# Key selection of a sparse attention layer: three query tiles searched each by itself with ScalarE counting and GpSimd keeping the bound, the other three in groups on VectorE

## The chip, the core and the metric

The kernel runs on one core of one Trainium2 chip. The core's engines are TensorE (PE, matmuls; PEld is its weight load), VectorE (DVE), ScalarE (ACT), GpSimd (POOL) and SyncE (SP, which issues transfers). Each engine takes its instructions in the order in which the program lists them, and waits at the first whose inputs are not there. The metric is the time of one execution on the device in microseconds, the median of several runs.

## What is computed

A decoder trunk of two layers over 1024 positions of 1024 features, in float32. The change lies in the second layer, a sparse attention: for each query an indexer scores all earlier keys, the 256 best are kept, and 16 heads attend to those alone.

```python
topk = min(TOPK_MAX, S // 4)                      # 256
...
rel = jax.nn.relu(jnp.einsum('bqhd,bkd->bqhk', qib, kif))
score = jnp.einsum('bqhk,bqh->bqk', rel, wib)
score = jnp.where(causal[None], score, -jnp.inf)
_, idx = lax.top_k(score, topk)
...
p = jax.nn.softmax(s, axis=-1)                    # over the selected keys
o = jnp.einsum('bqgjk,bqkgd->bqgjd', p, v_sel)
```

## The kernel before

**Tiles.** Queries are cut into eight tiles of 128. Query tile t sees (t+1)·128 keys, so tiles 0 and 1 need no selection (they have no more than 256 keys), and tiles 2 to 7 do, over 384 to 1024 keys.

**The search.** `index_tile(t)` computes the scores `sc_t` (128 queries by n keys). `topk` then finds, for each query, the 256th largest score by a binary search on the bits of the float: 16 steps on the high half word (`hw_t` holds it, int16), some work in between that puts the low half words of the keys at the threshold into `hw_t` (L1280 to L1297), and 16 steps on the low half (uint16). One step counts the keys above a bound `c2`, writes whether the count meets the limit (`hit`), and moves the bound. A count is either one VectorE instruction with an accumulator (L1236, output `jk`) or one ScalarE instruction, the sign of key minus bound with a sum (L1254, also into `jk`). The rest of a step is three small instructions on 128x(number of tiles): GpSimd takes half the step off the old bound (`cm`, L1249), VectorE compares the counts with the limit (L1260) and adds both (L1262; L1264 after the last step). After both searches each tile is finished on VectorE: a count, the two comparisons with the threshold (L1317, L1318), a running sum for ties (L1320), L1323 and L1326. L1326 writes the tile's mask into `hw_t`.

**Groups and where they count.** Tiles are searched in groups that share the small instructions. Group [3, 2] is searched early, while the scores of tiles 4 to 7 are computed, all of it on VectorE. Groups [7, 5] and [6, 4] come later, step by step in turn. In the first search of these ScalarE counts tiles 7 and 5 and VectorE 6 and 4; in the second ScalarE counts 7 and 4, and VectorE 5 and 6. VectorE does the small instructions of all groups.

**What lies around it.** TensorE has other work meanwhile: the scores (L1187), the query and key projections (`pj_qo`, `pj_ko`), which a fill queue spreads over the stage, the values `V_o`, and then the attention in units (query tile, key group, head pair). A unit of query tile t is named `o<t>_..`: scores `s_o` on TensorE, a masked row maximum on VectorE (L336, `st_o`), the exponential on ScalarE (L342), a scaling on GpSimd (L350), transposes `tp_o` on TensorE, their split into a high part on ScalarE (`ph_o`) and a low part on VectorE (`pl_o`), the product with the values, and the output's copies on ScalarE (L859, L861: `ah_o`, `a_o`), addition on GpSimd (L862) and split (`aoH` on ScalarE, `aoL` on GpSimd). The units of query tiles 0 and 1 need no mask from the search; those of tile 7 come next and need `hw_7` as L1326 leaves it, then the other tiles. The output weight is split into `woH` (ScalarE) and `woL` (VectorE or GpSimd); `held["sign"]` holds the first `woH` back until the last recorded sign is done. L1448 adds the attention's output to the residual.

**What sets the order.** The code is written in the order in which work is wanted; a scheduler that simulates the engines' times then fixes each engine's list. So a change of the search moves the instructions of everything around it as well. `topk` is a generator, one `yield` for each step, and the caller says which group steps when:

```python
    soon = topk([3, 2], ((), ()), 2, True)
...
    first, second = topk(TKA, TKACT, 0), topk(TKB, TKACT, 1)
    for _ in soon:
        next(first)
        next(second)
    while next(first, first) is not first:
        next(second)
    run(second)
```

## Time and profile before

| | us |
|---|---|
| median of three runs | 2592.92 (2591.56 to 2593.54) |
| the profiled execution, its own time | 2583.69 |
| its span in the trace | 2581.5 |
| TensorE busy | 2415.7 (94%) |
| VectorE busy | 1919.4 (74%) |
| ScalarE busy | 1275.2 (49%) |
| GpSimd busy | 937.9 (36%) |

The shares are averages over the whole span. The key selection lies between about 1339 and 1640 us, and there the picture is another: it has to be read from windows of that stretch. Rows further down give starts in us from the beginning of the span, then a duration, the engine, the line of the kernel, and what is written from what.

### The profile page before, as it was taken

What the parts mean: (1) busy time and instruction counts of PE and PEld (TensorE: products, weight loads), DVE (VectorE), ACT (ScalarE), POOL (GpSimd) and SP (SyncE); (2) the same over time, 40 slices, a digit from 0 to 9 for tenths busy, and PEclk for the clock granted to TensorE, in tenths of its full rate; (3) what the DMA queues carried; (4) which work ended last, traced back from release to release, by engine and by line L of the source; (5) the groups of instructions that cost most, each with busy time, mean ns of one, the idle gap of its engine ahead of it and who ended that gap; (6) DMA issues with size and microseconds to landing.
All of it is one profiled execution on the core that took longest, in us unless ns stands there. A gap on an engine that the chain in (4) does not pass through costs nothing.

```text
span 2581.5 us, 36095 instructions
## 1 busy us (share of the span) xinstructions
PE 2415.7 (94%) x12152; PEld 2024.3 (78%) x12152; DVE 1919.4 (74%) x3711; ACT 1275.2 (49%) x2395; POOL 937.9 (36%) x830
## 2 busy tenths in 40 slices
PE   8999999997999999999897886899988999999998
PEld 7888798886778877888686665799876788788887
DVE  5377765788665668788669999888856766688886
ACT  4354455555454453333434457777754544543333
POOL 2243344534333333244046434534441332324440
PEclk9999999998999999999999987999998999999999
DMA  7555565715254467542352334212342444684431
GB/s 256 157 172 150 156 187 150 216 34 200 89 175 135 149 239 253 163 147 98 114 136 70 110 108 90 82 50 74 83 176 94 165 149 150 213 317 147 146 115 66
DMA packets 160953, 373.14 MB, mean 145 GB/s; under 512 B 19329, under 2 KB 56449, under 8 KB 159745
## 3 DMA queue, kind: packets, MB, share of 16 engines
q1 hardware_dynamic: 160768, 370.85, 44.7%
q8 instruction: 96, 1.57, 0.3%
q14 instruction: 89, 0.72, 0.1%
HBM read 246.51 MB, written 123.73 MB: 143 GB/s over the span
## 4 chain that ended last, share of the span: by engine, by line
PE 71%; DVE 14%; DMA 6%; issue 4%; ACT 3%; POOL 1%; SPq 1%; DVEq 0%; POOLq 0%; ACTq 0%
PE dnA L702 13%; PE dnB L702 10%; PE upB L569 8%; PE pj_e L144 5%; PE upC L569 5%; PE upA L569 5%; PE o L144 4%; DVE jk L1236 3%; PE oo L144 3%; PE v L144 3%; PE tp_o L367 2%; PE dn_oe L144 2%; PE tp L367 2%; DMA K<-qk 1%; PE s L335 1%
## 5 line engine op out<-in xcount | busy, mean ns | idle before, releaser
L702 PE MATMUL dnA<-db,da 128*128 128x512 f32 x1536 | 354.5, 390 | 0.9 <-ACT db L100 0.9
L672 POOL TENSOR_TENSOR wr<-wr,wr 128x1024 f32<-128x1024 f32 x64 | 208.6, 3289 | 362.8 <-DVE db L101 319.5
L702 PEld LDWEIGHTS dnA<-db,da 128*128 128x128 f32 x1536 | 288.0, 188 | 62.9 <-ACT db L100 1.3
L702 PE MATMUL dnB<-db,da 128*128 128x512 f32 x1152 | 270.5, 395 | 5.7 <-DVE xd L709 5.7
L100 ACT CAST db<-wr 128x1024 fp32r<-128x1024 f32 x112 | 112.1, 1047 | 317.9 <-PE dnB L702 136.0
L702 PEld LDWEIGHTS dnB<-db,da 128*128 128x128 f32 x1152 | 217.9, 189 | 55.6 <-issue 6.1
L569 PE MATMUL upA<-B,wc 128*128 128x512 f32 x768 | 196.0, 403 | 11.5 <-ACT m L587 4.2
L101 DVE TENSOR_TENSOR da<-hr,da 128x1024 fp32r<-128x1024 f32 x112 | 187.5, 1706 | 19.4 <-ACT da L100 19.4
L569 PE MATMUL upB<-T,wc 128*128 128x512 f32 x768 | 187.8, 393 | 0.0
L569 PEld LDWEIGHTS upA<-B,wc 128*128 128x128 f32 x768 | 146.6, 192 | 48.6 <-ACT m L587 5.3
L101 DVE TENSOR_TENSOR wc<-ru,wc 128x512 fp32r<-128x512 f32 x148 | 125.5, 855 | 74.0 <-ACT wc L100 69.0
L536 POOL TENSOR_TENSOR ws<-ru 128x512 f32<-128x512 f32 x32 | 46.0, 1438 | 363.5 <-DMA ru<-in_ffn_up_dram 201.9
L101 DVE TENSOR_TENSOR db<-wr,db 128x1024 fp32r<-128x1024 f32 x112 | 164.8, 1510 | 14.3 <-ACT db L100 13.5
L100 ACT CAST wc<-ru 128x512 fp32r<-128x512 f32 x160 | 97.4, 619 | 157.1 <-DMA hid<-s 32.7
L569 PEld LDWEIGHTS upB<-T,wc 128*128 128x128 f32 x768 | 144.1, 188 | 32.7
L350 POOL TENSOR_SCALAR st_o<-st_o,am_o 128x128 f32<-128x128 f32 (+7 forms) x128 | 103.9, 814 | 137.2 <-DVE am_o L345 79.6
L342 ACT ACTIVATE st<-st,am 128x896 f32<-128x896 f32 (+7 forms) x128 | 99.3, 776 | 77.9 <-DVE am L336 76.2
L100 ACT CAST da<-hr 128x1024 fp32r<-128x1024 f32 x112 | 112.6, 1045 | 43.0 <-DMA hr<-hid 43.0
L350 POOL TENSOR_SCALAR st<-st,am 128x896 f32<-128x896 f32 (+3 forms) x96 | 74.7, 780 | 152.3 <-DVE am L345 145.6
L1236 DVE TENSOR_SCALAR_CACHE_REDUCE jk<-hw,tkf 128x512 bf16<-128x512 uint16 (+7 forms) x140 | 117.5, 865 | 1.0
L709 DVE TENSOR_TENSOR xd<-xd,dnA 128x512 f32<-128x512 f32 x128 | 84.7, 680 | 42.6 <-PE dnA L702 40.4
L342 ACT ACTIVATE st_o<-st_o,am_o 128x128 f32<-128x128 f32 (+7 forms) x128 | 99.3, 776 | 28.1 <-DVE am_o L336 24.6
(380 smaller groups left out, 6565.5 us busy)
## 6 DMA issues: line engine op xcount, KB each, us to landing
hr<-hid SPq DMA_DIRECT2D x112, 512.0 KB, 5.1
ru<-in_ffn_up_dram SPq DMA_DIRECT2D x70, 512.0 KB, 4.0
hid<-s SPq DMA_DIRECT2D x128, 256.0 KB, 3.3
wr<-in_ffn_down_dram SPq DMA_DIRECT2D x64, 512.0 KB, 5.2
hid<-c SPq DMA_DIRECT2D x96, 256.0 KB, 3.0
K<-qk SPq DMA_DIRECT2D x64, 192.0 KB, 4.6
x<-in_x_dram SPq DMA_DIRECT2D x16, 512.0 KB, 9.6
r_e<-in_w_qk_even_dram SPq DMA_DIRECT2D x16, 512.0 KB, 5.3
```

The source lines that it names most:

```text
L100: nc.scalar.copy(H, src)
L101: low.tensor_tensor(L, src, H.bitcast(F32), op=ALU.subtract)
L144: nc.tensor.matmul(self.ps, a, b, start=self.n == 0, stop=self.n == self.total - 1)
L342: nc.scalar.activation(st[:, :n], st[:, :n], AF.Exp, bias=last, scale=-1.0, accum_out=am[:, 2:3])
L350: nc.gpsimd.tensor_scalar(st[:, :n], st[:, :n], am[:, 3:4], 1.0, op0=ALU.mult, op1=ALU.mult)
L367: last_tp = nc.tensor.transpose(tp[:, a, s, :], strips[s][:, kb * P : (kb + 1) * P], ident)
L536: nc.gpsimd.tensor_tensor(s1, A21, A22, op=ALU.add)
L569: nc.tensor.matmul(ps, w[:, i, kb * P : (kb + 1) * P], b[:, j, kb, :], start=start and n == 0, stop=n == 11, skip_group_check=True,)
L672: nc.gpsimd.tensor_tensor(r, self.dr[x, i][1], self.dr[y, i][1], op=ALU.subtract)
L702: nc.tensor.matmul(ps, a[:, i, p, tk], b[:, j, p, :], start=start and m == 0, stop=m == 3 * NCP - 1, skip_group_check=True,)
L709: nc.vector.tensor_tensor(x[:, cs], x[:, cs], ps, op=ALU.add)
L1236: nc.vector.tensor_scalar(j[:, :n], src, thr, 0.0, op0=op, op1=ALU.add, accum_out=cnt[:, i : i + 1])
```

## The change

Tiles 7, 5 and 3 are each searched alone, as a group of one tile. ScalarE counts in all 32 steps (L1251, output `js`, one buffer); GpSimd computes `hit` (L1254) and the new bound (L1255) directly from the count, so that VectorE has no part in a step. Tiles 2 and [6, 4] remain groups that VectorE counts in both searches, with the three small instructions as before. `in_turn` steps several searches round robin: [3] and [2] early; [7], [6, 4] and [5] later. `held["sign"]` is now the last sign in the order of the program, which belongs to tile 5. The preparation before, between and after the searches stays on VectorE, but tiles 7, 5, 3 and 2 now do their small instructions each by itself. In all, VectorE counts 108 times rather than 140, ScalarE 96 times rather than 64; VectorE has 64 pairs of hit and bound rather than 96; GpSimd has 64 subtractions rather than 96, and 192 instructions more for hit and bound.

```diff
--- before.py
+++ after.py
@@ -50,8 +50,8 @@
 ODD = {"S": 2, "T": 3, "O": 2, "D": 1, "ph": 2}
 GATE = 7
 NPOOL = 2
-TKA, TKB = [7, 5], [6, 4]
-TKACT = (7, 5), (7, 4)
+ALONE = 7, 5, 3
+TOGETHER = [6, 4]
 N0, N1 = 14, 5
 WOL = 6
 IFILL = 0.6
@@ -1200,7 +1200,7 @@
         nc.gpsimd.tensor_tensor(dg, dg, caus[:, P : 2 * P], op=ALU.add)
         return si.ins
 
-    def topk(ts_, on_act, bi, early=False):
+    def topk(ts_, bi, early=False):
 
 
 
@@ -1209,6 +1209,7 @@
 
 
         m = len(ts_)
+        alone = m == 1 and ts_[0] in ALONE
         iv = O.tile([P, 3, m], I32, name=f"tki_{bi}")
         cn = O.tile([P, 13, m], F32, name=f"tkf_{bi}")
         Tt, Mx, ti = (iv[:, i, :] for i in range(3))
@@ -1216,11 +1217,10 @@
         for i, t in enumerate(ts_):
             nc.vector.memset(cols[:, i : i + 1], float((t + 1) * P))
 
-        def factors(on_act):
-            nc.vector.memset(mul, 1.0)
-            for i, t in enumerate(ts_):
-                if t in on_act:
-                    nc.vector.memset(mul[:, i : i + 1], 2.0)
+        def sign_out(t):
+            if early:
+                return O.tile([P, HALF], BF16, name=f"js_{bi}_{t}", tag="js", bufs=1)[:, : (t + 1) * P]
+            return A1.tile([P, T], BF16, name=f"js_{bi}_{t}", tag="tks", bufs=1)[:, : (t + 1) * P]
 
         k = [0]
 
@@ -1241,22 +1241,33 @@
         def half(t, i, dt):
             return sc[t].bitcast(dt).rearrange("p (n two) -> p n two", two=2)[:, :, i]
 
-        def search(tv, dt, on_act):
-
+        def search_alone(tv, dt):
+
+            (t,) = ts_
+            src = hw[t].bitcast(dt)
+            nc.gpsimd.tensor_scalar(c2, tv, 32767.5, None, op0=ALU.add)
+            for bit in range(15, -1, -1):
+                b = float(1 << bit)
+                held["sign"] = nc.scalar.activation(
+                    sign_out(t), src, AF.Sign, bias=c2, scale=-1.0, accum_out=cnt
+                )
+                nc.gpsimd.tensor_scalar(hit, cnt, lim, b, op0=ALU.is_le, op1=ALU.mult)
+                nc.gpsimd.tensor_scalar(
+                    c2 if bit else tv, hit, c2, b / 2, op0=ALU.add, op1=ALU.subtract
+                )
+                yield
+
+        def search(tv, dt):
+
+            if alone:
+                yield from search_alone(tv, dt)
+                return
             nc.vector.tensor_scalar(c2, tv, 32767.5, None, op0=ALU.add)
             for bit in range(15, -1, -1):
                 b = float(1 << bit)
                 nc.gpsimd.tensor_scalar(cm, c2, b / 2 if bit else 0.5, None, op0=ALU.subtract)
                 for i, t in enumerate(ts_):
-                    src = hw[t].bitcast(dt)
-                    if t in on_act:
-                        j = scratch()
-                        held["sign"] = nc.scalar.activation(
-                            j[:, : (t + 1) * P], src, AF.Sign, bias=c2[:, i : i + 1], scale=-1.0,
-                            accum_out=cnt[:, i : i + 1],
-                        )
-                    else:
-                        count(src, c2[:, i : i + 1], i, ALU.is_lt)
+                    count(hw[t].bitcast(dt), c2[:, i : i + 1], i, ALU.is_lt)
                 nc.vector.tensor_tensor(hit, cnt, lim, op=ALU.is_le)
                 if bit:
                     nc.vector.scalar_tensor_tensor(c2, hit, b, cm, op0=ALU.mult, op1=ALU.add)
@@ -1273,9 +1284,9 @@
             )
             nc.vector.tensor_tensor(hw[t], hi, j[:, :n], op=ALU.bitwise_xor)
         nc.vector.memset(t1, -32768.0)
-        factors(on_act[0])
+        nc.vector.memset(mul, 2.0 if alone else 1.0)
         nc.vector.scalar_tensor_tensor(lim, mul, -float(TOPK), cols, op0=ALU.mult, op1=ALU.add)
-        yield from search(t1, I16, on_act[0])
+        yield from search(t1, I16)
 
         nc.vector.tensor_scalar(off, t1, 0.0, None, op0=ALU.is_lt)
         nc.vector.tensor_scalar(sgn, off, -2.0, 1.0, op0=ALU.mult, op1=ALU.add)
@@ -1292,11 +1303,10 @@
             nc.vector.scalar_tensor_tensor(
                 hw[t].bitcast(U16), hw[t], thr, lo[:, :n], op0=ALU.is_equal, op1=ALU.mult
             )
-        factors(on_act[1])
         nc.vector.scalar_tensor_tensor(lim, cnt, -float(TOPK), mul, op0=ALU.add, op1=ALU.mult)
         nc.vector.tensor_tensor(lim, lim, cols, op=ALU.add)
         nc.vector.memset(t2, 0.0)
-        yield from search(t2, U16, on_act[1])
+        yield from search(t2, U16)
 
         nc.vector.tensor_copy(Tt, t1)
         nc.vector.tensor_copy(ti, t2)
@@ -1325,6 +1335,12 @@
             )
             nc.vector.tensor_tensor(hw[t].bitcast(BF16), eq[:, :n], below[:, :n], op=ALU.add)
 
+    def in_turn(*parts):
+        parts = list(parts)
+        while parts:
+            parts = [p for p in parts if next(p, parts) is not parts]
+            yield
+
     zero = O.tile([P, 1], BF16, name="zero")
     nc.vector.memset(zero, 0.0)
     run(index_queries(2 * P, HALF - 2 * P, range(2)))
@@ -1332,7 +1348,7 @@
     run(index_queries(2 * P, HALF - 2 * P, range(2, 4)))
     for t in (2, 3):
         index_tile(t)
-    soon = topk([3, 2], ((), ()), 2, True)
+    soon = in_turn(topk([3], 2, True), topk([2], 3, True))
     for _ in range(N0):
         next(soon)
     index_keys(1)
@@ -1457,13 +1473,10 @@
                     yield partial(front_c, t, gq, hp), partial(back_c, t, gq, hp)
 
     pipelined(units_c((0, 1)))
-    first, second = topk(TKA, TKACT, 0), topk(TKB, TKACT, 1)
+    later = in_turn(topk([7], 0), topk(TOGETHER, 1), topk([5], 4))
     for _ in soon:
-        next(first)
-        next(second)
-    while next(first, first) is not first:
-        next(second)
-    run(second)
+        next(later)
+    run(later)
     close_pool("odd_t", "odd_a")
 
     C = open_pool("odd_c", "left")
```

Line numbers of the changed kernel: the count is L1236 in both, the sign L1254 becomes L1251, the subtraction L1249 becomes L1268, hit L1260 becomes L1271, the bound L1262 becomes L1273, and from L1264 to L1326 of before it is 10 or 11 lines more.

ScalarE where the later groups begin their first search. A name such as `js_2_3` is the sign of search 2 over tile 3, `jk_0_4` the fourth count of group 0, `tkf` the group's small values; `rh_qo` and `wH_qo` are the query projection's. Before:

```order
L1254 ACTIVATE jk_0_3_14786,tkf_0_14770<-hw_7_11925,tkf_0_14770 128x1024
L1254 ACTIVATE jk_0_4_14788,tkf_0_14770<-hw_5_11923,tkf_0_14770 128x768
L1254 ACTIVATE jk_0_5_14814,tkf_0_14770<-hw_7_11925,tkf_0_14770 128x1024
L1254 ACTIVATE jk_0_6_14816,tkf_0_14770<-hw_5_11923,tkf_0_14770 128x768
L100 CAST rh_qo0_0_0_13377<-rq_qo0_0_0_13379 128x512
L100 CAST wH_qo0_3_13564<-r_qo0_3_13562 128x1024
L1254 ACTIVATE jk_0_7_14828,tkf_0_14770<-hw_7_11925,tkf_0_14770 128x1024
L1254 ACTIVATE jk_0_8_14830,tkf_0_14770<-hw_5_11923,tkf_0_14770 128x768
```

and in the changed kernel:

```order
L1251 ACTIVATE js_0_7_14861,tkf_0_14852<-hw_7_11925,tkf_0_14852 128x1024
L1251 ACTIVATE js_2_3_12688,tkf_2_12250<-hw_3_11921,tkf_2_12250 128x512
L100 CAST rh_qo0_0_0_13459<-rq_qo0_0_0_13461 128x512
L100 CAST wH_qo0_3_13646<-r_qo0_3_13644 128x1024
L1251 ACTIVATE js_4_5_14896,tkf_4_14887<-hw_5_11923,tkf_4_14887 128x768
L1251 ACTIVATE js_0_7_14900,tkf_0_14852<-hw_7_11925,tkf_0_14852 128x1024
L1251 ACTIVATE js_2_3_12710,tkf_2_12250<-hw_3_11921,tkf_2_12250 128x512
L100 CAST rh_qo0_0_512_13496<-rq_qo0_0_512_13498 128x512
L1251 ACTIVATE js_4_5_14911,tkf_4_14887<-hw_5_11923,tkf_4_14887 128x768
L103 ACTIVATE rh_qo0_1_0_13539<-pj_qo0_1_0_13514 128x512
```

Before, two signs of one group stand together and share one bound tile; now the signs of tiles 7, 3 and 5 follow each other in turn, each with its own bound, and the work of the projection lies among three signs a round.

ScalarE at the last sign. Before, it stands among the exponentials of query tile 0:

```order
L100 CAST ph_o0_1_0_0_14298<-tp_o0_1_0_0_14295 128x256
L342 ACTIVATE st_o0_2_1_1_14356,am_o0_2_1_1_14357<-st_o0_2_1_1_14356,am_o0_2_1_1_14357 128x128
L342 ACTIVATE st_o0_3_0_0_14375,am_o0_3_0_0_14376<-st_o0_3_0_0_14375,am_o0_3_0_0_14376 128x128
L1254 ACTIVATE jk_1_70_15285,tkf_1_14793<-hw_4_11922,tkf_1_14793 128x640
L100 CAST ph_o0_1_1_0_14330<-tp_o0_1_1_0_14327 128x256
L342 ACTIVATE st_o0_3_0_1_14384,am_o0_3_0_1_14385<-st_o0_3_0_1_14384,am_o0_3_0_1_14385 128x128
L859 COPY ah_o0_0_0_14266<-o_0_0_14228 64x256
L861 COPY a_o0_0_14265<-o_0_0_14228 64x256
```

and in the changed kernel behind the last output copies of query tile 1, and ahead of the output weight's casts:

```order
L1251 ACTIVATE js_0_7_15380,tkf_0_14852<-hw_7_11925,tkf_0_14852 128x1024
L859 COPY ah_o1_3_0_14841<-o_1_3_14813 64x256
L861 COPY a_o1_3_14840<-o_1_3_14813 64x256
L1251 ACTIVATE js_4_5_15391,tkf_4_14887<-hw_5_11923,tkf_4_14887 128x768
L100 CAST aoH_1_14584<-a_o1_2_14784 128x256
L859 COPY ah_o1_3_1_14845<-o_1_3_14813 64x256
L861 COPY a_o1_3_14840<-o_1_3_14813 64x256
L1251 ACTIVATE js_0_7_15395,tkf_0_14852<-hw_7_11925,tkf_0_14852 128x1024
L1251 ACTIVATE js_4_5_15406,tkf_4_14887<-hw_5_11923,tkf_4_14887 128x768
L100 CAST woH0_15479<-rwo_0_15483 128x512
```

So nearly all ScalarE work of the units of query tiles 0 and 1 now stands ahead of the last signs.

VectorE at the end of the search. Before, tile 4, the last, is finished between the row maxima of tile 7 and the last low parts of query tile 1:

```order
L336 ISA st_o7_0_0_1_15422,am_o7_0_0_1_15423<-s_o7_0_0_1_0_15424,hw_7_11925 128x512
L336 ISA am_o7_0_0_1_15423 128x1
L1320 SCALAR_TENSOR_TENSOR sc_4_12539<-jk_1_76_15339,zero_11960 128x640
L101 TENSOR_TENSOR pl_o1_3_0_0_14738<-tp_o1_3_0_0_14732,ph_o1_3_0_0_14737 128x512
L336 ISA st_o7_0_0_1_15422,am_o7_0_0_1_15423<-s_o7_0_0_1_1_15428,hw_7_11925,am_o7_0_0_1_15423 128x512
L336 ISA am_o7_0_0_1_15423 128x1
L1323 SCALAR_TENSOR_TENSOR jk_1_76_15339<-sc_4_12539,tkf_1_14793,jk_1_76_15339 128x640
L345 RECIPROCAL am_o7_0_0_0_15410<-am_o7_0_0_0_15410 128x1
L101 TENSOR_TENSOR pl_o1_3_1_0_14751<-tp_o1_3_1_0_14745,ph_o1_3_1_0_14750 128x512
L1326 TENSOR_TENSOR hw_4_11922<-jk_1_76_15339,jk_1_75_15338 128x640
L345 RECIPROCAL am_o7_0_0_1_15423<-am_o7_0_0_1_15423 128x1
L101 TENSOR_TENSOR woL0_15354<-rwo_0_15356,woH0_15352 128x512
```

In the changed kernel tile 5 is the last:

```order
L1333 SCALAR_TENSOR_TENSOR jk_1_76_15449<-sc_4_12573,tkf_1_14866,jk_1_76_15449 128x640
L1325 TENSOR_SCALAR tkf_4_14887<-tkf_4_14887 128x1
L1336 TENSOR_TENSOR hw_4_11922<-jk_1_76_15449,jk_1_75_15448 128x640
L1328 TENSOR_SCALAR jk_4_6_15466<-sc_5_12863,tkf_4_14887 128x768
L1330 SCALAR_TENSOR_TENSOR sc_5_12863<-jk_4_6_15466,zero_11960 128x768
L101 TENSOR_TENSOR pl_o7_0_0_0_15606<-tp_o7_0_0_0_15600,ph_o7_0_0_0_15605 128x512
L1333 SCALAR_TENSOR_TENSOR jk_4_6_15466<-sc_5_12863,tkf_4_14887,jk_4_6_15466 128x768
L101 TENSOR_TENSOR pl_o7_0_0_2_15622<-tp_o7_0_0_2_15616,ph_o7_0_0_2_15621 128x512
L1336 TENSOR_TENSOR hw_5_11923<-jk_4_6_15466,jk_4_5_15465 128x768
L101 TENSOR_TENSOR pl_o7_0_0_4_15635<-tp_o7_0_0_4_15629,ph_o7_0_0_4_15634 128x512
L101 TENSOR_TENSOR woL0_15481<-rwo_0_15483,woH0_15479 128x512
L101 TENSOR_TENSOR woL1_15482<-rwo_0_15483,woH1_15480 128x512
```

The low parts of query tile 1 now stand ahead of all finishing; the finishing of tiles 7, 6, 4 and 5, 52 rows with four row maxima of tile 7 and two of its low parts among them, follows in one piece, and the low halves of the output weight stand behind it. From the residual addition L1448 on the order is the same in both kernels.

## Rows read from the trace of the kernel before

**Rows 1.** The first part of the page: span, and busy time, share and instructions of each engine.

```profile
span 2581.5 us, 36095 instructions
PE 2415.7 (94%) x12152; PEld 2024.3 (78%) x12152; DVE 1919.4 (74%) x3711; ACT 1275.2 (49%) x2395; POOL 937.9 (36%) x830
```

**Rows 2.** Four windows of 20 us through the key selection and behind it: start and end of the window, its length, then busy us (x instructions) of each engine, the granted TensorE clock, the DMA share and GB/s.

```profile
1380.00:1400.00 20.00, 11.47 (x47) 8.29 (x47) 19.76 (x29) 9.61 (x20) 16.05 (x12) 0.92 0.16 54
...
1560.00:1580.00 20.00, 11.46 (x55) 8.60 (x53) 18.74 (x88) 17.64 (x55) 5.32 (x19) 0.74 0.70 136
...
1600.00:1620.00 20.00, 13.78 (x62) 11.30 (x63) 19.81 (x55) 13.61 (x39) 18.05 (x24) 0.67 0.14 27
...
1660.00:1680.00 20.00, 20.00 (x129) 17.96 (x129) 17.26 (x47) 16.05 (x31) 9.35 (x8) 1.00 0.20 73
```

**Rows 3.** VectorE's groups from 1339 to 1640 us, shapes apart: the counts of the search by width, and the two updates that end each step (L1260 hit, L1262 the new bound).

```profile
L1260 DVE TENSOR_TENSOR tkf<-tkf 128x2 f32<-128x2 f32 x96 | 24.0, 260 | 0.2
L1262 DVE SCALAR_TENSOR_TENSOR tkf<-tkf 128x2 f32<-128x2 f32 x90 | 21.6, 250 | 2.5
...
L1236 DVE TENSOR_SCALAR_CACHE_REDUCE jk<-hw,tkf 128x896 bf16<-128x896 int16 x17 | 19.4, 1139 | 0.0
L1236 DVE TENSOR_SCALAR_CACHE_REDUCE jk<-hw,tkf 128x768 bf16<-128x768 uint16 x17 | 17.2, 1009 | 0.3
L1236 DVE TENSOR_SCALAR_CACHE_REDUCE jk<-hw,tkf 128x640 bf16<-128x640 int16 x17 | 14.8, 872 | 0.0
L1236 DVE TENSOR_SCALAR_CACHE_REDUCE jk<-hw,tkf 128x512 bf16<-128x512 int16 x17 | 12.6, 742 | 0.3
...
L1236 DVE TENSOR_SCALAR_CACHE_REDUCE jk<-hw,tkf 128x384 bf16<-128x384 uint16 x17 | 10.3, 608 | 0.0
```

**Rows 4.** ScalarE's groups from 1339 to 1640 us: the sign counts by width and type, a weight cast, a rounding of the query projection, the exponentials of the units of query tiles 1 and 0, and one of their two output copies.

```profile
L1254 ACT ACTIVATE jk<-hw,tkf 128x1024 bf16<-128x1024 int16 x16 | 18.4, 1149 | 49.5 <-DVE tkf L1262 28.6 <-DVE tkf L1282 7.0 <-DVE tkf L1260 5.7
...
L1254 ACT ACTIVATE jk<-hw,tkf 128x768 bf16<-128x768 int16 x16 | 14.7, 921 | 0.3 <-DVE tkf L1264 0.3
...
L100 ACT CAST wH_qo<-r_qo 128x1024 fp32r<-128x1024 f32 x8 | 8.3, 1044 | 5.0 <-PE pj_ko L144 4.8 <-PE pj_qi L144 0.2
L342 ACT ACTIVATE st_o<-st_o,am_o 128x256 f32<-128x256 f32 x16 | 8.1, 508 | 6.5 <-DVE am_o L336 6.3
...
L103 ACT ACTIVATE rh_qo<-pj_qo 128x512 fp32r<-128x512 f32 x12 | 6.8, 578 | 0.0
...
L342 ACT ACTIVATE st_o<-st_o,am_o 128x128 f32<-128x128 f32 x16 | 6.3, 394 | 0.5 <-DVE am_o L336 0.5
...
L859 ACT COPY ah_o<-o 64x256 f32<-64x256 f32 x16 | 5.9, 366 | 4.0 <-PE o L144 3.6
```

**Rows 5.** GpSimd's groups from 1420 to 1640 us: the bound's subtraction (L1249), the addition and the scalings of the units, the low part of their output.

```profile
L1249 POOL TENSOR_SCALAR tkf<-tkf 128x2 f32<-128x2 f32 x78 | 17.4, 227 | 85.7 <-DVE tkf L1262 64.6 <-DVE tkf L1260 9.0 <-DVE tkf L1264 6.7
L862 POOL TENSOR_TENSOR a_o<-a_o,ah_o 64x256 f32<-64x256 f32 x16 | 14.5, 905 | 1.5 <-ACT a_o L861 0.8
L350 POOL TENSOR_SCALAR st_o<-st_o,am_o 128x256 f32<-128x256 f32 x16 | 13.1, 826 | 3.3 <-DVE am_o L345 2.8 <-PE tp_o L367 0.2
...
L350 POOL TENSOR_SCALAR st_o<-st_o,am_o 128x128 f32<-128x128 f32 x16 | 8.1, 507 | 9.3 <-PE o L144 2.5 <-DVE am_o L345 2.4 <-DVE pl_o L101 1.2
L101 POOL TENSOR_TENSOR aoL<-a_o,aoH 128x256 fp32r<-128x256 f32 x8 | 6.8, 849 | 1.7 <-ACT aoH L100 1.7
```

**Rows 6.** VectorE's own sequence in the index stage: start, duration, line.

```profile
1387.02 0.75 DVE L1236 TENSOR_SCALAR_CACHE_REDUCE jk<-hw,tkf 128x512 bf16<-128x512 int16 x1
...
1387.69 0.61 DVE L1236 TENSOR_SCALAR_CACHE_REDUCE jk<-hw,tkf 128x384 bf16<-128x384 int16 x1
...
1391.82 5.24 DVE L1262 SCALAR_TENSOR_TENSOR tkf<-tkf 128x2 f32<-128x2 f32 x1
```

**Rows 7.** GpSimd's sequence at the same place.

```profile
1392.67 2.08 POOL L1196 TENSOR_TENSOR sc<-sc,ri 128x896 f32<-128x896 f32 x1
1394.70 2.34 POOL L101 TENSOR_TENSOR wL_qo<-r_qo,wH_qo 128x1024 fp32r<-128x1024 f32 x1
```

**Rows 8.** ScalarE's sequence: the first sign of the second search of tile 7, the first exponential of the units of tile 0, and the last sign of the kernel before.

```profile
1520.01 1.15 ACT L1254 ACTIVATE jk<-hw,tkf 128x1024 bf16<-128x1024 uint16 x1 [6.48 <-DVE tkf L1296]
...
1568.15 0.40 ACT L342 ACTIVATE st_o<-st_o,am_o 128x128 f32<-128x128 f32 x1
...
1578.42 0.82 ACT L1254 ACTIVATE jk<-hw,tkf 128x640 bf16<-128x640 uint16 x1
```

**Rows 9.** VectorE's sequence: the first work on tile 7's keys, then the finishing of tile 7 (L1318 to L1326), the first low halves of the output weight, and the first residual addition of the layer.

```profile
1416.96 2.49 DVE L1271 TENSOR_SCALAR jk<-sc 128x1024 int16<-128x1024 int16 x2
...
1584.87 1.22 DVE L1318 TENSOR_SCALAR jk<-sc,tkf 128x1024 bf16<-128x1024 f32 x1
...
1587.76 2.27 DVE L1320 TENSOR_TENSOR_SCAN sc<-jk,zero 128x1024 f32<-128x1024 bf16 x1
...
1591.73 1.39 DVE L1323 SCALAR_TENSOR_TENSOR jk<-sc,tkf,jk 128x1024 bf16<-128x1024 f32 x1
...
1594.44 0.95 DVE L1326 TENSOR_TENSOR hw<-jk,jk 128x1024 bf16<-128x1024 bf16 x1
...
1628.32 5.58 DVE L101 TENSOR_TENSOR woL<-rwo,woH 128x512 fp32r<-128x512 f32 x6
...
1650.38 0.68 DVE L1448 TENSOR_TENSOR xo<-xo,oo 128x512 f32<-128x512 f32 x1
```

## The prediction

> **What bounds the kernel now.** I read the page first [rows 1]: TensorE is busy in 94% of the span, VectorE in 74%, so over the whole run VectorE is not the limit. Then the windows of the key selection [rows 2]: from 1380 to 1620 us VectorE is busy 18.7 to 19.8 of every 20 us, while TensorE has 11.5 to 13.8 in the three windows shown and its granted clock falls to 0.67; from 1660 us TensorE is busy 20.00 of 20 at full clock. So between the score stage and 1650 us VectorE sets the pace, TensorE is often idle, and a microsecond gained or lost there is one of the whole kernel. ScalarE is not free there: 9.6 of 20 in the index stage, 17.6 of 20 at 1560. GpSimd reaches 16.1 and 18.1 of 20 in two of these windows. The question is whether work can go to these two without their becoming the pace. After 1650 us, at the residual addition [rows 9], the two kernels have the same order, so I compare what lies ahead of that row in three pieces, in us of the trace of before.
>
> **What leaves VectorE.** A count of 512 keys takes 0.74, and the next count starts 0.67 later [rows 3, 6]; with the same 0.07 off, 384, 640, 768 and 896 take 0.54, 0.80, 0.94 and 1.07. The two small updates have means of 0.26 and 0.25 [rows 3]; those means hold blocked ones from the index stage, and among other work I take 0.2 for the pair (two starts overlap as the counts do).
>
> *Index stage, to 1417 us* (first work on tile 7's keys, [rows 9]). 15 counts of tile 3 leave: 15 x 0.67 = 10. ScalarE gets as many signs of 512. Their time is not in the trace; from 1.15 for 1024 and 0.92 for 768 [rows 4] I estimate 0.69. ScalarE has room for 10 us among its relus. But each step is now sign, hit, bound, sign, and GpSimd's two instructions stand in its list behind additions of 2.08 and weight splits of 2.34 [rows 7]. A sign that stands ahead of relus then holds the scores up. Gain between 10 and a loss of 2; I take 7, nearer to the full gain, as GpSimd has a fifth of its time free even there.
>
> *From 1417 us to the first sign of tile 7's second search at 1520* [rows 8]: 103 us. In the changed order VectorE's rows between these points hold 16 counts of 512 fewer (10.7) and 16 pairs fewer (3.2), and some small set-up rows more, as four searches have them singly: 13 less, so 90 if nothing waits. ScalarE's rows of this piece hold 17 signs of 512 (11.8), 16 of 1024 (18.4), 16 of 768 (14.7), seven weight casts of 1.04 (7.3) and 15 roundings of 0.58 (8.7) [rows 4]: 61 us, 3.8 for each of 16 rounds. VectorE's own rounds (384, 896, 640 and two pairs, 2.8, and some 0.3 of the projection's work) are 3.1 to 3.3. Nothing in VectorE's groups needs a sign. But GpSimd's subtraction for a VectorE group (mean 0.23, [rows 5]) stands in the same list as the hits, which wait for signs; so VectorE is drawn to ScalarE's round. 16 x 0.5 = 8 lost of the 13; between 3 and 13. Sum: 5 gained.
>
> *From 1520 to the residual addition at 1650.4*: 130.4 us before. I build the new piece from three stretches.
> First, to the first exponential of query tile 0, before 48 us [rows 8]. In the changed order only nine rounds of the second search stand ahead of it. A round on VectorE is 1.07 + 0.80 + 0.4 for a lone pair, in which the second update waits for the first = 2.3; ScalarE's is 1.15 + 0.92. Nine are 21; the preparation of the other tiles and the values ahead of them make 12: 33 us. Over all 16 rounds VectorE loses a 768, gains a 640 and loses a pair, 16 x (0.14 + 0.2) = 5.5 saved.
> Second, to the last sign. The last eight or nine signs of tiles 7 and 5 now stand among the units of tiles 0 and 1, the very last behind their output copies. ScalarE's rows in this stretch: 17 signs 17.5, 32 exponentials with the reading of their sums 14.4 to 16, 32 copies of 0.37, 11.7, and 23 casts of some 0.35, about 8: 52 us. GpSimd's: scalings 13.1 + 8.1, additions 14.5, low parts 6.8 [rows 5], 17 pairs of hit and bound at 2 x 0.21, 7, and 1 of subtractions: 51. VectorE's are 40. Two full lists that wait for each other: a sign needs the bound, which stands behind scalings in GpSimd's list; a scaling needs VectorE's reciprocal, that an exponential, that stands behind a sign. 52 would be both at full use. Before, ScalarE in such a stretch has 17.6 of 20 and then 13.6 [rows 2]; 52 at these is 59 and 76. I take 64, nearer to the denser window, as signs are long and need only one partner.
> Third, from the last sign to the residual addition. Before, the last sign is at 1578.4 [rows 8], and tiles 7, 5, 6 and 4 are finished by VectorE among the units, where others work beside it. Now all four stand behind the units. Tile 7's finishing from its rows [rows 9] is 1.2 (L1318) + 2.2 (L1320) + 1.3 (L1323) + 0.9 (L1326), with a count of 1.2 and L1317 with 0.6: 7.4; tiles 6, 5 and 4 by width 6.6, 6.1 and 6.1; with the small rows, four row maxima of 0.7 and two low parts: 33. TensorE has six score matmuls of tile 7 meanwhile and then waits. Then follow the low halves of the output weight (their high halves wait for tile 5's last sign, and have these 33 us to arrive in); from these to the residual addition it was 22 us [rows 9], of which three go with work done already: 19. Sum 52, between 45 and 55.
> 33 + 64 + 52 = 149 against 130.4: 18.6 lost.
>
> **The sum.** -7 - 5 + 18.6 = +6.6 on the profiled execution of 2583.7, so 2590.3. That execution lies 9.2 below the median of 2592.92; with the same distance the forecast is 2599 us. VectorE is relieved of 10 + 13 + 5.5 = 28.5 us, and idles about 35: 3 in the index stage, 8 in the first search, 24 among the units. Its own range, from -10 to +2, -10 to 0, and +8 to +28 taken as independent, is 2588 to 2611.
>
> **Rivals.**
> *VectorE stays the pace* (0.27). GpSimd's small instructions are short (0.23, [rows 5]), and ScalarE's idle before a sign is mostly waiting for VectorE's bound (28.6 of 49.5 us, [rows 4]), a wait that the change removes. Then the index stage gives 9, the first search 10, and the units run at the 17.6 of 20 of the dense window (59) with a finishing of 46: 33 + 59 + 46 - 130.4 = +7.6. Together -11.4, with 9.2: 2581; with no idle at all -28.5, 2564. Against it speaks GpSimd's 18.1 of 20 at 1600 us. The Trainium skill, Perfetto Trace Analysis, section Optimizing Scalar/DVE Operations, says that with a saturated VectorE moving work to ScalarE may make sense; that is this case, and no run here shows yet whether ScalarE's list takes it.
> *The late signs cost more* (0.19). If ScalarE gets only the 13.6 of 20 of the window at 1600, the stretch of the units is 76 and the piece costs 31; with 5 gained in the index stage and 2 lost in the first search, +28: 2621. It decides from a ScalarE share below two thirds in that stretch.
> *GpSimd blocks VectorE* (0.05). An update of 128x2, 0.25 in the mean, took 5.24 from 1391.82 and ended as GpSimd's split ended at 1397.04 [rows 6, 7], with its inputs done. If each of the 192 new instructions blocked VectorE for its own 0.21, 40 us would come back against 28.5 saved: 2592.9 + 11.5 = 2604. Against it: the 78 subtractions of the same size ran between counts whose mean stayed 0.742 in 17 [rows 3, 5]. The Trainium skill, SBUF — State Buffer, section on the two separate sides, states the rule: VectorE and GpSimd share a port pair that one holds for a whole instruction. The 5.24 us agree with it; the counts beside the small instructions show nothing of it.
> *No difference* (0.10). The idle moves from VectorE to the finishing and back, and both kernels reach the residual addition within 5 us of each other: 2593.
>
> **How the numbers follow.** The forecast has the remaining 0.39. A measurement can tell about 0.2%, 5.2 us, from no change: 2587.7 and 2598.1. Of the forecast's own range a little under half lies within these, the rest mostly above: 0.02 faster, 0.16 same, 0.21 slower. With the rivals: faster 0.26 + 0.02 = 0.28; same 0.16 + 0.10 + 0.01 of the first rival = 0.27; slower 0.21 + 0.19 + 0.05 = 0.45. The range of 8 in 10 cuts the first rival at 2577 and reaches to the second: 2577 to 2621.
>
> **What would show it.** Right: in the windows from 1417 to 1500 VectorE falls from nearly 20 to about 18 of 20, and GpSimd's hits wait for ScalarE; the last sign comes after the last output copy of query tile 1; between the first exponential of tile 0 and that sign VectorE is busy about two thirds; behind it VectorE finishes four tiles in some 33 us with TensorE nearly idle and its clock down; the residual addition comes near 1657 us. Wrong on the fast side: VectorE remains above 19 of 20 up to the units, and the residual addition comes before 1645. Wrong on the slow side: the stretch of the units lasts over 70 us. If the small updates of VectorE have a mean over 0.4 from 1420 on, it is the third rival.

## The result and the profile after

The changed kernel takes 2607.24 us in the median of four runs (2606.64 to 2611.85), the kernel before 2592.73 (2591.56 to 2593.54): a ratio of 1.0062, 95% interval 1.0049 to 1.0075, so 14.5 us slower. The forecast was 2599, the range 2577 to 2621.

The profiled execution of the changed kernel took 2606.64 us. Its page, span and engines as in [rows 1]:

```profile
span 2604.5 us, 36229 instructions
PE 2417.6 (93%) x12152; PEld 2022.5 (78%) x12152; DVE 1890.8 (73%) x3604; ACT 1298.0 (50%) x2459; POOL 985.2 (38%) x996
```

VectorE has 28.6 us less to do, as worked out ahead (28.5), and the kernel is slower. The windows of the changed kernel, with the columns of [rows 2]; those of 20 us answer to the rows there, the longer ones are cut at the landmarks that the prediction used:

```profile
1380.00:1400.00 20.00, 14.85 (x56) 12.39 (x57) 16.29 (x30) 12.13 (x26) 13.10 (x17) 0.83 0.08 27
...
1424.00:1537.00 113.00, 99.46 (x410) 77.83 (x409) 92.95 (x263) 65.09 (x127) 78.79 (x157) 0.95 0.32 110
1500.00:1520.00 20.00, 16.51 (x65) 12.92 (x64) 4.21 (x9) 14.93 (x29) 17.93 (x32) 0.91 0.38 135
1569.00:1626.00 57.00, 36.41 (x160) 28.53 (x160) 34.97 (x159) 52.97 (x154) 40.38 (x93) 0.68 0.22 47
1600.00:1620.00 20.00, 13.20 (x63) 9.54 (x62) 8.05 (x27) 19.54 (x54) 17.51 (x35) 0.82 0.12 26
1626.00:1655.00 29.00, 10.66 (x31) 6.98 (x32) 28.90 (x57) 7.74 (x15) 4.05 (x5) 0.50 0.00 1
1660.00:1680.00 20.00, 18.10 (x89) 12.47 (x90) 16.26 (x40) 14.79 (x26) 10.71 (x9) 1.00 0.40 134
```

From 1424 to 1537 (tile 7's preparation to its second search) VectorE is busy 92.95 of 113 us; it had work for 90 by the prediction. In 1500 to 1520 it does 4.21 of 20. From 1569 to 1626, the units with the last signs, ScalarE is full (52.97 of 57) and VectorE has 34.97. From 1626 to 1655 VectorE is full, TensorE has 10.66 of 29, with a granted clock of 0.50, the lower of its two levels (1.2 of 2.4 GHz). From 1660 TensorE has 18.10 of 20 again, at full clock.

The landmarks as in [rows 8, 9]: on ScalarE the first sign of tile 7's second search, the first exponential of query tile 0, the last sign;

```profile
1536.95 1.15 ACT L1251 ACTIVATE js<-hw,tkf 128x1024 bf16<-128x1024 uint16 x1 [8.46 <-DVE tkf L1298]
...
1569.41 0.40 ACT L342 ACTIVATE st_o<-st_o,am_o 128x128 f32<-128x128 f32 x1 [1.57 <-DVE am_o L336]
...
1625.06 0.93 ACT L1251 ACTIVATE js<-hw,tkf 128x768 bf16<-128x768 uint16 x1
```

on VectorE the first work on tile 7's keys, the mask of tile 7 and that of tile 5, the first low halves of the output weight, and the residual addition:

```profile
1423.86 1.63 DVE L1282 TENSOR_SCALAR jk<-sc 128x1024 int16<-128x1024 int16 x3 [3.67 <-POOL sc L1200]
...
1634.96 0.69 DVE L1336 TENSOR_TENSOR hw<-jk,jk 128x1024 bf16<-128x1024 bf16 x1
...
1654.44 0.55 DVE L1336 TENSOR_TENSOR hw<-jk,jk 128x768 bf16<-128x768 bf16 x1
...
1655.51 3.69 DVE L101 TENSOR_TENSOR woL<-rwo,woH 128x512 fp32r<-128x512 f32 x6
...
1674.02 0.68 DVE L1464 TENSOR_TENSOR xo<-xo,oo 128x512 f32<-128x512 f32 x1
```

The residual addition stands at 1674.0 against 1650.4 in [rows 9], 23.6 us later, which is more than the 14.5 of the medians. The profiled execution of before was 9 us faster than its median; e0 below is a second profile of the same kernel.

### The profile page after: what moved, and what is told of

It reads as the page before. It is cut to its first block, busy times and chain, and to the rows that moved or that the text cites. A ratio compares the mean times of both kernels' runs of the same rounds, so it can differ in the third digit from the quotient of the medians.

```text
span 2604.5 us, 36229 instructions
## 1 busy us (share of the span) xinstructions
PE 2417.6 (93%) x12152; PEld 2022.5 (78%) x12152; DVE 1890.8 (73%) x3604; ACT 1298.0 (50%) x2459; POOL 985.2 (38%) x996
## 4 chain that ended last, share of the span: by engine, by line
PE 71%; DVE 13%; DMA 6%; ACT 4%; issue 4%; POOL 1%; SPq 1%; DVEq 0%; POOLq 0%; ACTq 0%
PE dnA L702 13%; PE dnB L702 10%; PE upB L569 8%; PE pj_e L144 6%; PE upC L569 5%; PE upA L569 5%; PE o L144 4%; PE oo L144 3%; PE v L144 3%; DVE jk L1236 2%; PE dn_oe L144 2%; PE tp_o L367 2%; PE tp L367 2%; PE s L335 1%; PE s L334 1%
## 5 line engine op out<-in xcount | busy, mean ns | idle before, releaser
L569 PEld LDWEIGHTS upA<-B,wc 128*128 128x128 f32 x768 | 146.8, 192 | 50.8 <-ACT m L587 6.3
L350 POOL TENSOR_SCALAR st_o<-st_o,am_o 128x128 f32<-128x128 f32 (+7 forms) x128 | 95.7, 752 | 160.3 <-DVE am_o L345 104.3
L1251 ACT ACTIVATE js<-hw,tkf 128x1024 bf16<-128x1024 uint16 (+4 forms) x96 | 89.5, 932 | 55.1 <-POOL tkf L1255 34.4
```

The lines of the kernel that those rows point to most:

```text
L350: nc.gpsimd.tensor_scalar(st[:, :n], st[:, :n], am[:, 3:4], 1.0, op0=ALU.mult, op1=ALU.mult)
L569: nc.tensor.matmul(ps, w[:, i, kb * P : (kb + 1) * P], b[:, j, kb, :], start=start and n == 0, stop=n == 11, skip_group_check=True,)
L1251: held["sign"] = nc.scalar.activation(sign_out(t), src, AF.Sign, bias=c2, scale=-1.0, accum_out=cnt)
```

## The experiments

In all of them the time is compared with the kernel before, run on the same chip in the same hours (medians of 2590.8 to 2592.3 us). "Tk" stands for tile k. Pieces are durations between the landmarks above, from the profile of each run: *first* from T7's preparation to T7's second search, *units* from the first exponential to the last sign, *tail* from the last sign to the residual addition; the last sign counts to the end of reading its sum.

| run | median us | ratio (95%) | T7 prepared at | first | second search to first exponential | units | tail |
|---|---|---|---|---|---|---|---|
| before, first profile | 2592.73 | | 1417.0 | 103.0 | 48.1 | 11.2 | 71.0 |
| before, second profile (e0) | 2595.85, one run | | 1424.8 | 103.0 | 48.1 | 11.2 | 71.9 |
| the change | 2607.24 | 1.0062 (1.0049 to 1.0075) | 1423.9 | 113.1 | 32.5 | 56.7 | 47.9 |
| e1 T3 alone only | 2591.38 | 1.0007 (0.9997 to 1.0017) | 1426.5 | 93.4 | 53.6 | 17.6 | 66.0 |
| e2 T7, T5 alone only | 2600.17 | 1.0036 (1.0024 to 1.0049) | 1423.7 | 104.5 | 47.3 | 37.8 | 51.5 |
| e3 small on VectorE | 2606.16 | 1.0061 (1.0049 to 1.0073) | 1428.0 | 101.7 | 46.8 | 42.6 | 50.7 |
| e5 group first | 2591.14 | 1.0007 (0.9998 to 1.0015) | 1422.7 | 108.4 | 35.8 | 47.3 | 38.2 |
| e6 own scratch | 2608.48 | 1.0071 (1.0058 to 1.0084) | 1431.2 | 123.6 | 26.0 | 57.3 | 34.9 |
| e8 group first, T3 and T2 grouped | 2591.18 | 1.0003 (0.9994 to 1.0012) | 1419.6 | 103.7 | 58.6 | 4.1 | 64.4 |
| e7b e8 with T5's second search on VectorE | 2597.38 | 1.0024 (1.0015 to 1.0032) | 1424.1 | 101.6 | 64.2 | last sign earlier | 71.9 from the exponential |
| e9 e5 with one head on GpSimd | 2582.90 | 0.9960 (0.9948 to 0.9971) | 1427.7 | 102.2 | 38.0 | 36.4 | 45.6 |
| e10 group finished first | 2600.83 | 1.0033 (1.0021 to 1.0045) | 1423.0 | 113.1 | 32.5 | 61.4 | 34.1 |
| e11 e5 with the first search's small on VectorE | 2582.23 | 0.9960 (0.9947 to 0.9972) | 1427.0 | 96.8 | 50.8 | 16.4 | 55.2 |
| e13 e9 and e11 together | 2574.85 | 0.9936 (0.9922 to 0.9951) | 1419.9 | 88.5 | 59.0 | 2.1 | 68.5 |

**e0, the kernel before once more.** No edit.

> The kernel before, unchanged, profiled once more: the first profile of it was 9 us below its median. If that gap lies in the index stage, the first work on tile 7's keys starts near 1424 us here (as in the four kernels profiled since) and not at 1417, and the residual addition near 1658; if it lies elsewhere, the start is again near 1417. Time 2584 to 2595 us.

VectorE's first work on T7's keys and the residual addition:

```profile
1424.82 2.43 DVE L1271 TENSOR_SCALAR jk<-sc 128x1024 int16<-128x1024 int16 x2
...
1658.99 0.68 DVE L1448 TENSOR_TENSOR xo<-xo,oo 128x512 f32<-128x512 f32 x1
```

The pieces after T7's preparation are those of the first profile to 0.9 us; of the gap of 8.6 us at the residual addition, 7.9 lie in the index stage, in two executions of one program. So the start of T7's preparation is known only to some 8 us from one profile, and I compare the pieces behind it. Against this profile the change is 1.0 us earlier at T7's preparation and 15.0 later at the residual addition, near the 14.5 of the medians. The two executions as wholes differ by 10.8, since e0 took 4.2 us longer behind the residual addition, where the order of work is the same; so these comparisons are good to some microseconds.

**e1 and e2, one part of the change each.**

```diff
-ALONE = 7, 5, 3                                   # e1
+ALONE = (3,)
+TKACT = (7, 5), (7, 4)        # groups [7, 5] and [6, 4] count as before
...
-    later = in_turn(topk([7], 0), topk(TOGETHER, 1), topk([5], 4))
+    later = in_turn(topk([7, 5], 0), topk([6, 4], 1))
...
-ALONE = 7, 5, 3                                   # e2
+ALONE = 7, 5
-    soon = in_turn(topk([3], 2, True), topk([2], 3, True))
+    soon = topk([3, 2], 2, True)
```

> Only tile 3 is searched by itself (ScalarE counts, GpSimd moves the bound), tile 2 by itself on VectorE; the later groups are [7, 5] and [6, 4] as in the kernel before. Theory A (both places lose: the chain of sign, hit and bound through two lists in order costs some 7 us in the index stage and as much in the first searches, and the late finishing some 10 us): the early loss stays and the late one goes, 2597 to 2602 us. Theory B (the whole loss is the late finishing behind the last sign; the early part gains what VectorE is relieved of): 2573 to 2583. Theory C (GpSimd's small instructions block VectorE, in proportion to their number, 64 of 192): about 2597, with VectorE's counts of 384 longer than their 0.61.

> Tiles 7 and 5 are searched alone, tiles 3 and 2 in one group on VectorE as in the kernel before. Theory A: the index stage is as before, the first searches wait less with two signs a round in place of three, the finishing remains late: 2598 to 2603 us, with 28 to 34 us from the last sign to the end of the finishing. Theory B: all of the loss is left, 2605 to 2610. Theory C: two thirds of it, about 2602, with longer counts.

e1 is as fast as before; A and C expected 2597 or more, B 2583 or less, and all three fall. T3's search alone shortens *first* by 9.6 us, but the pieces behind it are 6.0 longer. e2 keeps 9 us of the loss, as A said: its *first* is near that of before, its finishing late (32.0 us from the last sign to the last mask). Neither part alone loses 14.5. The windows of *first* in e1 and in e2, columns as above:

```profile
1426.00:1520.00 94.00, 83.37 (x341) 65.56 (x339) 90.87 (x266) 60.56 (x121) 60.87 (x105) 0.96 0.31 107
```

```profile
1424.00:1528.00 104.00, 83.83 (x329) 65.94 (x328) 103.22 (x290) 48.31 (x84) 64.04 (x117) 0.89 0.31 107
```

e1 has three signs a round in its first searches as the change has, and VectorE counts the same tiles, but only T3's hit and bound are on GpSimd: *first* is 93.4 in place of 113.1, with GpSimd at 60.87 in place of 78.79. So three signs a round do not lengthen it by themselves. e2's *first* has another limit: T3's counts are on VectorE there, and VectorE is busy 103.22 of 104 us.

**e3, the small instructions on VectorE.**

```diff
-                nc.gpsimd.tensor_scalar(hit, cnt, lim, b, op0=ALU.is_le, op1=ALU.mult)
-                nc.gpsimd.tensor_scalar(
+                nc.vector.tensor_scalar(hit, cnt, lim, b, op0=ALU.is_le, op1=ALU.mult)
+                nc.vector.tensor_scalar(
```

> The changed kernel with hit and bound of tiles 7, 5 and 3 on VectorE in place of GpSimd: 192 small instructions more on VectorE, about 0.2 to 0.4 us a pair, 19 to 36 us of work, and none on GpSimd. Theory A: a sign's bound no longer stands behind GpSimd's splits and additions of 1.3 to 2.4 us, so the index stage and the first searches get 7 to 14 us back, but VectorE pays for it where it is full: 2598 to 2610 us, and the idle of VectorE before tile 7's preparation and at the end of the first searches is under half of what it is in the changed kernel. Theory C: more than 10 us are gained, 2597 or less. Theory B: 2605 or more, since the finishing is as late.

The window from T7's preparation to its second search in e3, columns as above:

```profile
1428.00:1530.00 102.00, 88.90 (x347) 69.68 (x346) 96.97 (x330) 59.18 (x114) 43.14 (x49) 0.92 0.31 106
```

*first* falls by 11.4 us with GpSimd at 43.14 of 102 in place of 78.79 of 113: the chain through GpSimd is what lengthened it. Part of this is that T3's steps come earlier: of its 32 signs 18 lie ahead of T7's preparation in e3, and 13 in the change. The time stays at 2606: 3 us go in the last pieces, where VectorE pays, and 4 in the index stage, which is within what one profile can tell; the other 4 are there at the residual addition, and the medians show 1.1 of them. C fell: nothing was gained, and the counts have the same mean in both (605 ns for 384 keys).

**e5, e6 and e10, the order of the finishing.**

```diff
-    later = in_turn(topk([7], 0), topk(TOGETHER, 1), topk([5], 4))          # e5
+    later = in_turn(topk(TOGETHER, 1), topk([7], 0), topk([5], 4))
...
-            ... name=f"jk_{bi}_{k[0]}", tag="tk", bufs=3)                   # e6
+            ... name=f"jk_{bi}_{k[0]}", tag="tkg" if bi == 1 else "tk", bufs=3)
...
-        parts = list(parts)                                                 # e10
+        parts, n = list(parts), [0]
         while parts:
+            n[0] += 1
+            if n[0] == 33 and len(parts) == 3:
+                parts = [parts[1], parts[0], parts[2]]
             parts = [p for p in parts if next(p, parts) is not parts]
```

> The changed kernel with the searches in turn as [6, 4], [7], [5] in place of [7], [6, 4], [5]; nothing else. The scratch tiles rotate in program order, so in the changed kernel the finishing of 6 and 4, whose search is done 34 us before the last sign, stands behind that of 7. Theory A: VectorE finishes 6 and 4 while it waits among the units, some 13 us leave the piece behind the last sign: 2594 to 2599 us. Theory B: the same or more, 2593 to 2597. Rival: TensorE waits for the mask of tile 7 and for the output weight behind the last sign in either case, and the place of 6 and 4 changes nothing: 2604 to 2609.

> The changed kernel with scratch tiles of its own for the searches of 6 and 4, in the program order of the changed kernel. Theory D (the rotation of the shared scratch tiles holds the finishing of 6 and 4 behind that of 7, and that is the whole loss): their finishing stands among the units, and the time is that of the run with the group first, 2588 to 2595 us. Theory E (the place of the group in the program, not the scratch, decides, by the order in which things reach GpSimd and ScalarE): 2600 to 2609.

> The changed kernel with its own turns [7], [6, 4], [5] through all steps of both searches; only the finishing is issued for 6 and 4 first, then 7 and 5. Theory D' (the finishing of 6 and 4 behind the last sign costs about 10 us of the piece from the last sign to the residual addition, 48 us in the changed kernel and 35 to 38 in the two runs that finish 6 and 4 earlier; the rest of what the group first gained lies in the turns): the piece from tile 7's preparation to its second search stays near 113 us, that from the last sign to the residual addition becomes 35 to 40: 2595 to 2600 us. Rival (the turns are all): 2603 to 2609.

e5 takes back all of the loss, 2 us more than the best that I expected, and not where I expected it: the tail is 9.7 us shorter, *first* and *units* 4.7 and 9.4, and the piece between these two 3.3 longer. e6 moves the finishing of T6 and T4 ahead in the same way (tail 34.9), and is not faster. Its start of T7's preparation, its first sign of the second search, and its residual addition:

```profile
1431.15 1.15 DVE L1282 TENSOR_SCALAR jk<-sc 128x1024 int16<-128x1024 int16 x2
...
1554.74 1.15 ACT L1251 ACTIVATE js<-hw,tkf 128x1024 bf16<-128x1024 uint16 x1 [14.39 <-DVE tkf L1293]
...
1672.99 0.68 DVE L1464 TENSOR_TENSOR xo<-xo,oo 128x512 f32<-128x512 f32 x1
```

ScalarE waits 14.39 us there for VectorE's preparation of T7's second search: without the shared scratch VectorE runs on with the group, and *first* becomes 123.6. So D's mechanism was right (the rotation held the finishing back) and its sum wrong; what frees VectorE's list in one place lets the scheduler fill it in another. e10 changes the finishing alone. Its first sign of the second search and its residual addition:

```profile
1536.06 1.15 ACT L1251 ACTIVATE js<-hw,tkf 128x1024 bf16<-128x1024 uint16 x1 [8.45 <-DVE tkf L1298]
...
1664.08 0.69 DVE L1467 TENSOR_TENSOR xo<-xo,oo 128x512 f32<-128x512 f32 x1
```

*first* is 113.1 as in the change, the tail 34.1 against 47.9, and the units, with that finishing among them, 4.7 longer: 9.1 gained in the trace, 6.4 between the medians. That is the price of the late finishing. D' was right in the pieces (*first* near 113, the tail 35 to 40 by forecast and 34.1), and the time lies 0.8 above its range.

**e8 and e7b, signs ahead of the units.** e8 is e5 with T3 and T2 grouped (the edit of e2). In e7b T5's second search is counted on VectorE:

```diff
-            if alone:
+            if alone and (dt == I16 or ts_[0] != 5):
                 yield from search_alone(tv, dt)
...
+        if ts_[0] == 5:
+            nc.vector.memset(mul, 1.0)
```

> The changed kernel with the searches in turn as [6, 4], [7], [5], and with tiles 3 and 2 in one group on VectorE: the last signs stand ahead of the units but for three. Theory D with late signs as a second, smaller cost: neither is left, and VectorE is relieved of the second search's 16 counts of 768 less 16 of 640 and of 16 pairs: 2582 to 2590 us. Theory F (signs of 7 and 5 cost what they cost wherever they stand, as ScalarE and GpSimd are full): 2592 to 2600, as with tiles 7 and 5 alone.

> As the run with the group first and tiles 3 and 2 on VectorE, but tile 5's second search is counted on VectorE: ScalarE has 16 signs of 768 less, VectorE 16 counts of 768 and 16 lone pairs more, about 20 us. No sign stands among the units. If VectorE sets the pace from the second search on, 10 us or more over the run without this (2594 to 2605 us); if ScalarE and the chain through GpSimd do, the same or less (2582 to 2590).

e8 is as fast as before, between what D and F expected, so it decides neither: its last sign comes 4.1 us after the first exponential and not 56.7 as in the change, but that exponential comes 162 us after T7's preparation and not 146, as VectorE is full again up to it (18.9 to 20.0 in every 20 us from 1420 to 1600). e7b costs 6.2 us more, where 10 or more were expected if VectorE sets the pace and none if it does not: it does, though not for all of the 20 us that were added.

**e9, e11 and e13, a shorter list for GpSimd.**

```diff
-NPOOL = 2                                         # e9, e13
+NPOOL = 1
...
+            eng = nc.vector if dt == I16 else nc.gpsimd                     # e11, e13
-                nc.gpsimd.tensor_scalar(hit, ...
+                eng.tensor_scalar(hit, ...
```

> The run with the group first, and in the score stage GpSimd weights one of the eight heads in place of two; VectorE takes the other. Theory G (in the index stage GpSimd's list, with the hits and bounds of tile 3 among its scalings and additions, holds the last scores of tile 7, so VectorE's relief there is worth nothing): the first work on tile 7's keys comes 4 to 8 us earlier than the 1422.7 there, 2583 to 2588 us. Rival: VectorE, which has a pass of 1.15 more for each tile, or TensorE sets the stage, and the start is at 1421 to 1428: 2589 to 2596.

> The run with the group first, with hit and bound of the lone tiles on VectorE in the first of the two searches and on GpSimd in the second. Theory H (in the first searches the chain of a lone tile waits in GpSimd's list, behind weight splits and rotations of 1.3 to 2.4 us, and VectorE waits for it at the end): the piece from tile 7's preparation to its second search falls from 108 to 98 to 103 us, the rest stays: 2580 to 2587. Rival (VectorE pays for 96 more small instructions what the chain gains): 2589 to 2596.

> The two best runs in one: the group [6, 4] first, hit and bound of the lone tiles on VectorE in the first search and on GpSimd in the second, and one head of the scores weighted on GpSimd in place of two. If their gains of 8 to 9 us over the run with the group first lie at different places (index stage and first searches), 2573 to 2579 us; if both come from the same shorter list of GpSimd in the first searches, 2580 to 2585; if VectorE is full with both, over 2585.

Windows of the first searches, e11 and then e13:

```profile
1427.00:1524.00 97.00, 80.09 (x323) 63.23 (x322) 94.62 (x312) 58.21 (x113) 50.64 (x81) 0.91 0.31 107
```

```profile
1420.00:1508.00 88.00, 71.91 (x297) 56.05 (x295) 85.23 (x304) 58.78 (x114) 51.40 (x84) 0.96 0.28 101
```

H held in its time, 8.9 us less at 2582.2, and roughly in its place: *first* falls by 11.6, to 1.2 below H's range, and the pieces behind it, each of another length, are 1.1 longer in sum. e9's time is what G said to 0.1, its place not: T7's preparation stands at 1427.7, no earlier, and in the profile *first* is shorter (102.2 against 108.4). With the 8 us by which that start differs between executions, G stays open. e13 adds both gains, 2574.85 where the two taken off e5's time give 2574.0. Its landmarks, T7's preparation, the second search and the residual addition:

```profile
1419.87 0.69 DVE L1283 TENSOR_SCALAR jk<-sc 128x1024 int16<-128x1024 int16 x1
...
1508.33 1.15 ACT L1252 ACTIVATE js<-hw,tkf 128x1024 bf16<-128x1024 uint16 x1 [0.81 <-DVE hw L1304]
...
1637.87 0.69 DVE L1465 TENSOR_TENSOR xo<-xo,oo 128x512 f32<-128x512 f32 x1
```

e13 is the fastest, 0.9936 of the kernel before: *first* takes 88.5 us, and VectorE is busy 85.23 of 88 and GpSimd 51.40.

## Why the prediction was right in direction and short in size

| term | forecast | measured, against the second profile of before |
|---|---|---|
| index stage | -7 | -1.0 |
| first searches | -5 | +10.1 |
| second search to first exponential | 33 | 32.5 |
| units to the last sign | 64 | 56.7 |
| last sign to the residual addition | 52 | 47.9 |
| these three, less those of before | +18.6 | +5.9 |
| sum | +6.6 | +15.0 |

That it came out slower, and within the range, is in good part luck. The forecast had gains of 12 us ahead of the second search and a loss of 18.6 behind it; measured were a loss of 9.1 ahead and one of 5.9 behind. The three errors, 6, 15 and -13 us, leave 8. With the gains as forecast and the last pieces as measured, the kernel would have been 6 us faster.

**The step that failed** is the loss in the first searches, 8 us of 13. VectorE's own work there was nearly right (90, measured 92.95), but VectorE idles 20 us in place of 8. The prediction drew VectorE to ScalarE's round of 3.8 us, and gave GpSimd's list no length of its own in this piece. VectorE isn't held to ScalarE's round: from 1440 to 1500 it is busy 19.5 to 20.0 of every 20 us, runs ahead through [6, 4] and T2, and then stands still. Its waits from 1500 to 1524 (us in total, times, longest):

```profile
DVE rl_qo L104 <- ACT rh_qo L103: 13.1, 2, 10.2
DVE tki L1312 <- POOL tkf L1255: 4.2, 1, 4.2
```

What it waits for is ScalarE's rounding of the projection, which stands in ScalarE's list behind signs, and these wait for GpSimd's bounds (ScalarE's waits from 1440 to 1524):

```profile
ACT js L1251 <- POOL tkf L1255: 23.8, 14, 5.3
```

The prediction's sign of being right, GpSimd's hits waiting for ScalarE, is the other way round. From 1424 to 1537 the first of these rows is ScalarE's wait for bounds, the second GpSimd's for signs:

```profile
ACT js L1251 <- POOL tkf L1255: 28.3, 15, 5.3
...
POOL tkf L1254 <- ACT js L1251: 4.6, 6, 1.6
```

Where the prediction prices hit and bound, it goes by the row of the subtraction: 0.23 in the mean, 0.21 taken for each. GpSimd's groups from 1420 to 1540 in the changed kernel, and four of its instructions in a row:

```profile
L1254 POOL TENSOR_SCALAR tkf<-tkf 128x1 f32<-128x1 f32 x53 | 19.8, 374 | 13.3 <-ACT js L1251 10.7
L1255 POOL TENSOR_SCALAR tkf<-tkf 128x1 f32<-128x1 f32 x54 | 19.3, 357 | 4.2
...
L1268 POOL TENSOR_SCALAR tkf<-tkf 128x2 f32<-128x2 f32 x16 | 3.8, 236 | 3.4 <-DVE tkf L1273 2.4
```

```profile
1510.76 0.29 POOL L1254 TENSOR_SCALAR tkf<-tkf 128x1 f32<-128x1 f32 x1
1511.14 0.30 POOL L1255 TENSOR_SCALAR tkf<-tkf 128x1 f32<-128x1 f32 x1
1511.53 0.30 POOL L1254 TENSOR_SCALAR tkf<-tkf 128x1 f32<-128x1 f32 x1
1511.92 0.30 POOL L1255 TENSOR_SCALAR tkf<-tkf 128x1 f32<-128x1 f32 x1
```

A hit or a bound takes 0.30 when nothing disturbs it, 0.36 to 0.37 in the mean, and the next that depends on it starts 0.39 later: 0.78 a step, not 0.42. For the 107 in this stretch I estimate from this some 19 us more in GpSimd's list (107 times 0.39 less 0.21), which was busy 78.79 of 113, with splits of 2.4 among them. e3 and e11 show that GpSimd's list is the cause: with these instructions on VectorE the piece is 11.4 and 11.6 shorter, and VectorE's wait for the rounding, 13.1 us in the change and 7.2 in e5, is 1.0 in e3 and gone in e11. How much of it is the price of a step, and how much the splits that stand between, no run tells apart.

**The index stage** gave 1 and not 7. 10 us of counts left VectorE, but the five accumulations of T7's scores took 6.6 us in both profiles of before and 12.5 now; the first row is before, the second after, VectorE's groups up to 1424:

```profile
L1193 DVE SCALAR_TENSOR_TENSOR sc<-ri,wi,sc 128x1024 f32<-128x1024 f32 x5 | 6.6, 1322 | 0.2
```

```profile
L1193 DVE SCALAR_TENSOR_TENSOR sc<-ri,wi,sc 128x1024 f32<-128x1024 f32 x5 | 12.5, 2500 | 0.2
```

and VectorE waited 6.4 us for GpSimd's last score additions, against 2.8 before. How much of that holds in other executions stays open, since the start of T7's preparation moves by 8 us by itself.

**The late signs** went as forecast in kind: ScalarE's 52 us of work were 52.97, behind them TensorE had 10.66 of 29 us, and VectorE finished four tiles in those 29 (forecast 33). ScalarE was used to 93%, above the 88% of the dense window, so 56.7 and not 64. The finishing was forecast too long: its sum has 6.6, 6.1 and 6.1 for tiles 6, 5 and 4 "by width", where the widths give 6.5, 5.6 and 4.6. The two long waits of TensorE around the last sign, for ScalarE's cast and for VectorE's row maximum of T7:

```profile
1626.64 0.80 PE L144 MATMUL oo<-woH,aoH 128*128 128x512 f32 x1 [6.92 <-ACT woH L100]
1637.84 0.80 PE L334 MATMUL s_o<-Ko,qo_t 128*128 128x512 f32 x1 [10.40 <-DVE am_o L336]
```

**The rivals.** "VectorE stays the pace" gave +7.6 for the last pieces, which did +5.9, but its gains of 19 ahead of them did not come; it is what the whole kernel does in e13 once GpSimd's list is short. "The late signs cost more" failed: ScalarE was full, not at two thirds. "GpSimd blocks VectorE": the counts did not lengthen, as the prediction had it, the small updates from 1420 on had means of 0.17 to 0.31, below the 0.4 of its sign, and e3 gained nothing in all; the blocking that there is stands in the long accumulations above. Of the runs with two heads weighted on GpSimd, the five take 12.5 us in all that have T3's hit and bound there (the change, e1, e5, e6, e10), and 6.4 to 6.7 in the others. In e3, which has the same signs of T3:

```profile
L1193 DVE SCALAR_TENSOR_TENSOR sc<-ri,wi,sc 128x1024 f32<-128x1024 f32 x5 | 6.7, 1337 | 0.1
```

But while the longest of them ran, 6.29 us in the rows at the end of this document, GpSimd did a rotation, a split and an addition and neither a hit nor a bound; in e3 the accumulations begin 4 us after the split's end. So by these rows T3's steps lengthen them by where they come to run, beside GpSimd's long instructions, and not by blocking of their own; no run tries the two apart.
